# Writing out the hand-over from the up to the down product, holding late jobs behind splits, and grouping wide and narrow matmuls

## The chip, the cores and the metric

The kernel runs on one core of one Trainium2 chip. The metric is device time in microseconds: the median of three runs, 2068.24 us (2066.79 to 2068.33). The engines are named as the profile names them: PE (TensorE, with PEld for its weight loads), DVE (VectorE), ACT (ScalarE), POOL (GpSimd), and SP, whose queue issues nearly all transfers. Each engine runs its own list of instructions in order and waits on semaphores for the others.

## The reference

One residual block over 512 rows of 2048 columns in float32. What matters here is the second half, the feed-forward part:

```python
h2 = rmsnorm(x, g_mlp[l])
u = jax.nn.relu(jnp.einsum('bsd,df->bsf', h2, w_up[l]))
x = x + jnp.einsum('bsf,fd->bsd', u * u, w_down[l])
return rmsnorm(x, g_final)
```

`w_up` is 2048 x 8192 and `w_down` 8192 x 2048. Before it come an input projection, two kinds of attention with eight heads each, and an output projection.

## The kernel before, in words

**Numbers in two parts.** Every float32 operand is split into a high part (rounded to the fp32r type, a cast on ACT, L71) and a low part (the rest, a subtraction on DVE, L72). A full product is three matmuls, high by high, high by low, low by high: `mm3`, L104 to L106.

**Seven products in place of eight.** Both large matrix products use a Strassen-like scheme on 2 x 2 blocks: seven products of sums and differences of blocks, numbered 1 to 7. The sums of the weight blocks are formed on DVE in place (for the up weights L564 to L570, for the down weights L918 to L924).

**The up product** is cut into 32 units of 256 hidden columns, `Unit(u)`. Its left side F (both time halves in two parts) stays in SBUF. From unit 2 on, products 1, 2, 4, 6 and 7 join two of the three matmuls: one 512 columns wide takes high and low parts of F together against the high weights (L594), one 256 wide takes the high part of F against the low weights (L595). They stand in one loop over eight chunks, so wide and narrow alternate. Products 3 and 5 use `mm3` with 256 columns. The accumulators are the PSUM tiles `psa`, `psb`, `psc`. The copies out of them are on ACT (L622 to L627), the sums on DVE (L633 to L636), relu and square on ACT (L639, L641).

**Who sets the order.** Most of the program is ordered by a scheduler with its own estimates of time, which may move an instruction far ahead of where it is written. For the up units from 2 on, the orders on PE, ACT and DVE are written out by hand instead: a list `steps` of (unit, product) and a loop that, for each step, makes the cast for the step three ahead (L1019), the low part for two ahead (L1025), the copies and sums of the step behind, a piece of a job, and the matmuls. SP's order stays with the scheduler.

**Jobs.** The squared hidden values of a pair of units are turned into the left side of the second product by `form_steps`: a difference on DVE, a cast into a buffer `st` on ACT (L868), the low part on DVE (L870), and a store to memory `ufd` through SP (L873). Two units at the end are stored by `store_last` as `su` into `usd` (L885). `st`, `su` and `xr` share three buffers with the tag `wraw`.

**The down product** runs over eight groups of units: two of three units, six of four. In each group there are two column blocks (`db` 0 and 1), and in each the seven products in the order 1, 5, 2, 6, 3, 7, 4 (`second`). `load_b` loads four blocks of `w_down` (`wd`, L911), `load_uf` the left side of a product (`uf`, L900). A product takes its weights two units at a time: a split, then 12 matmuls for two units or 6 for one. So a product is 18 matmuls in the first two groups and 24 later. Product 1 accumulates over all groups in PSUM (`M1`, in the profile `m`). The others go into one of two `accd` buffers and from there into `M` in SBUF: by a copy on ACT in the first group (L941), by an addition on DVE in the later ones (L943). The eight residual pieces `xr` are loaded (L949), scaled on ACT (L951) and added on DVE (L952) by `add_residual`, one per column block from the fourth group on as the program is written. The stores left over (`jobs`) are written in the second group, at every other product.

**The hand-over.** Behind the written-out loop, the scheduler orders the loads for the first group, product 1 of the first column block, and products 4 and 3 of the last up unit.

Of the kernel before, what the change touches and what calls it, by code (L numbers as in the profile page):

```python
# [14 lines left out]
P = 128  # L15
NT = 512
# [10 lines left out]
NU = DFF // P // 2  # L27
# [8 lines left out]
def block_kernel(ctx, tc, x, g_attn, w_in, b_f, g_out_sb, g_out_fox, w_out, g_mlp, w_up, w_down, g_final, y):  # L36
# [505 lines left out]
    class Unit:  # L542
# [30 lines left out]
        def room(self):  # L573
            return [w.rearrange("p (a b) -> p a b", b=P) for w in hi_lo(2 * NT)]

        def parts(self, p):
            src = self.source(p)
            hi, lo = self.room()
            split(hi, lo, src)
            return hi, lo  # L580

        def multiply(self, p, parts):
# [7 lines left out]
            if self.both and p not in (5, 3):  # L590


                for a in PAIRS:
                    pe.matmul(ps, hi[:, a, :], f_both(p, a), start=a == PAIRS[0] and p == 1, stop=False, skip_group_check=True)  # L594
                    ins = pe.matmul(ps[:, 2 * P:], lo[:, a, :], f_parts(p, a)[0], start=False, stop=a == PAIRS[-1],  # L595
                                    skip_group_check=True)
                return ins
# [304 lines left out]
    def load_b(group, db):  # L902
# [9 lines left out]
                b.append(t_)  # L912
        return b

    def second(p, b, db, n, first):
        b11, b12, b21, b22 = b
        if p == 5:
# [9 lines left out]
        for u0 in range(0, n, 2):  # L927
            m = min(2, n - u0)
            hi, lo = (w.rearrange("p (a b) -> p a b", a=m) for w in hi_lo(m * NT))
            split(hi, lo, src[:, u0:u0 + m, :])  # L930
            for t in range(2):
                ts = slice(t * P, (t + 1) * P)
                for u in range(m):
                    mm3(ps[:, t, :], uf[p][:, 0, u0 + u, ts], uf[p][:, 1, u0 + u, ts], hi[:, u, :], lo[:, u, :],
                        u0 + u == 0 and (first or p != 1), u0 + u == n - 1)
        if p == 1:
            return
        if first:
# [43 lines left out]
    while squares:  # L982
# [16 lines left out]
    todo += [(q, hidden[0], 0) for q in A_ORDER]  # L999


    made = {2: Unit(2)}
    steps = [(u - i, p, n) for u in range(2, NU)
             for n, (i, p) in enumerate(((0, 1), (1, 4), (0, 5), (1, 3), (0, 6), (0, 2), (0, 7))) if u - i >= 2]
    srcs, rooms = {}, {}

    def at_step(k):
# [7 lines left out]
    def step_cast(k):  # L1015
        w, p = at_step(k)
        if w is not None and k not in rooms:
            rooms[k] = w.room()
            act.copy(rooms[k][0], srcs[k])  # L1019

    def step_low(k):
# [15 lines left out]
    with tc.manual_schedule(engines={pe.engine, act.engine, dve.engine}):  # L1037
# [5 lines left out]
        for k in range(len(steps)):  # L1043
            n = steps[k][2]
            if n == 0 and steps[k][0] + 1 < NU:
                made[steps[k][0] + 1] = Unit(steps[k][0] + 1)
            w, p = at_step(k - 1)
            if w is not None:
                w.copies(p)
# [23 lines left out]
                w.multiply(p, rooms.pop(k))  # L1073
    w, p = at_step(len(steps) - 1)
    w.finish(p)

    old = w
    for p in ORDER:
        load_uf(p, GROUPS[0])
    b_first = load_b(GROUPS[0], 0)  # L1080
    second(1, b_first, 0, GROUPS[0][1], True)
    for p in (4, 3):
        old.product(p)
    if going:
        for _ in going[0][0]:
            pass
# [34 lines left out]
    for g, group in enumerate(GROUPS):  # L1121
        last = g == len(GROUPS) - 1
        for db in range(2):
# [150 lines left out]
```

## Time and profile before

| | |
|---|---|
| median of three runs | 2068.24 us |
| profiled execution, its time | 2068.4 us |
| profiled execution, its span | 2066.7 us |
| granted TensorE clock, mean | 0.997 |
| matmuls | 10802 |
| up product with its written-out order | about 820 to 1430 us |
| hand-over | about 1410 to 1470 us |
| down product | about 1437 to 2010 us |

The page gives the busy time of each engine and the costliest groups of instructions. The answers on waits say who waited for whom; the timeline lists instructions with start and duration. A matmul's recorded duration overlaps the start of the next, so the rate of matmuls is read from starts, counts in a window, or differences between mean durations. A table of windows shows busy time and counts for PE, PEld, DVE, ACT and POOL, then the granted clock, the share of the DMA engines and their rate. The prediction shows the lines.

### The profile page before, as it was taken

What the parts mean: (1) busy time and instruction counts of PE and PEld (TensorE: products, weight loads), DVE (VectorE), ACT (ScalarE), POOL (GpSimd) and SP (SyncE); (2) the same over time, 40 slices, a digit from 0 to 9 for tenths busy, and PEclk for the clock granted to TensorE, in tenths of its full rate; (3) what the DMA queues carried; (4) which work ended last, traced back from release to release, by engine and by line L of the source; (5) the groups of instructions that cost most, each with busy time, mean ns of one, the idle gap of its engine ahead of it and who ended that gap; (6) DMA issues with size and microseconds to landing.
All of it is one profiled execution on the core that took longest, in us unless ns stands there. A gap on an engine that the chain in (4) does not pass through costs nothing.

```text
span 2066.7 us, 27642 instructions
## 1 busy us (share of the span) xinstructions
PE 2041.9 (99%) x10802; PEld 1759.7 (85%) x10802; DVE 1641.8 (79%) x1772; ACT 1092.4 (53%) x1578; POOL 54.6 (3%) x76
## 2 busy tenths in 40 slices
PE   9999999999999999999999999999999999999998
PEld 8887888888888889999999999998788888888886
DVE  6667754566578578898998999998688888989895
ACT  6434433445455466667767666676643444433443
POOL 0000000000010000000000000000000000000003
PEclk9999999999999999999999999999999999999999
DMA  7877743223238882666666666667755764764732
GB/s 246 291 273 271 254 132 83 77 87 82 71 95 264 298 261 96 210 185 186 215 200 187 210 197 191 207 197 280 264 199 198 260 238 160 279 233 144 272 115 82
DMA packets 258851, 402.46 MB, mean 195 GB/s; under 512 B 9456, under 2 KB 154912, under 8 KB 251168
## 3 DMA queue, kind: packets, MB, share of 16 engines
q1 hardware_dynamic: 257760, 398.56, 58.8%
q10 hardware_dynamic: 960, 2.13, 0.3%
q8 instruction: 85, 1.39, 0.3%
q14 instruction: 46, 0.38, 0.1%
HBM read 307.85 MB, written 92.80 MB: 194 GB/s over the span
## 4 chain that ended last, share of the span: by engine, by line
PE 82%; DMA 7%; DVE 7%; ACT 2%; issue 2%; SPq 0%; POOL 0%; ACTq 0%; DVEq 0%
PE psa L594 11%; PE accd L104 7%; PE accd L106 7%; PE accd L105 7%; PE psa L595 5%; PE accq L104 4%; PE accq L105 4%; PE accq L106 4%; PE psc L106 3%; PE psc L105 3%; PE psc L104 3%; PE psb L594 3%; DMA wsums<-mixed 2%; DMA mixed<-in_w_out_dram 2%; PE accv L104 2%
## 5 line engine op out<-in xcount | busy, mean ns | idle before, releaser
L594 PE MATMUL psa<-f,wh 128*128 128x512 f32 x728 | 258.1, 396 | 0.0
L71 ACT CAST wh<-wd 128x1024 fp32r<-128x1024 f32 (+1 forms) x136 | 134.8, 999 | 182.6 <-PE accd L106 111.7
L595 PE MATMUL psa<-f,wl 128*128 128x256 f32 x728 | 204.2, 281 | 0.0
L1025 DVE TENSOR_TENSOR wl<-wu,wh 128x1024 fp32r<-128x1024 f32 x156 | 190.1, 1218 | 14.0 <-ACT wh L1019 13.9
L104 PE MATMUL accq<-hH,wh 128*128 128x512 f32 x512 | 200.4, 391 | 0.4 <-DVE vl L75 0.4
L105 PE MATMUL accq<-hL,wh 128*128 128x512 f32 x512 | 200.2, 391 | 0.0
L106 PE MATMUL accq<-hH,wl 128*128 128x512 f32 x512 | 200.2, 391 | 0.0
L1019 ACT CAST wh<-wu 128x1024 fp32r<-128x1024 f32 x156 | 165.0, 1058 | 55.4 <-PE psc L105 41.9
L72 DVE TENSOR_TENSOR wl<-wd,wh 128x1024 fp32r<-128x1024 f32 (+1 forms) x136 | 155.3, 1152 | 41.1 <-ACT wh L71 40.7
L104 PE MATMUL accd<-wh,uf 128*128 128x512 f32 x436 | 169.8, 390 | 1.5 <-issue 0.9
L105 PE MATMUL accd<-wl,uf 128*128 128x512 f32 x436 | 169.6, 389 | 0.0
L106 PE MATMUL accd<-wh,uf 128*128 128x512 f32 x436 | 169.6, 389 | 0.0
L72 DVE TENSOR_TENSOR wl<-wraw,wh 128x1024 fp32r<-128x1024 f32 (+2 forms) x101 | 119.5, 1184 | 57.1 <-ACT wh L71 51.3
L594 PEld LDWEIGHTS psa<-f,wh 128*128 128x128 f32 x728 | 136.6, 188 | 31.4
L71 ACT CAST wh<-wraw 128x1024 fp32r<-128x1024 f32 (+2 forms) x101 | 101.8, 1009 | 107.3 <-PE accq L105 68.5
L71 ACT CAST wx<-wd 128x1024 fp32r<-128x1024 f32 (+1 forms) x88 | 87.4, 1000 | 118.5 <-PE accd L106 71.0
L595 PEld LDWEIGHTS psa<-f,wl 128*128 128x128 f32 x728 | 137.6, 189 | 0.0
L72 DVE TENSOR_TENSOR wx<-wd,wx 128x1024 fp32r<-128x1024 f32 (+1 forms) x88 | 100.9, 1153 | 23.1 <-ACT wx L71 22.7
L104 PE MATMUL accd<-wx,uf 128*128 128x512 f32 x284 | 111.6, 393 | 4.9 <-ACT m L941 4.9
L104 PEld LDWEIGHTS accq<-hH,wh 128*128 128x128 f32 x512 | 96.2, 188 | 20.3 <-PE accv L106 0.8
L106 PEld LDWEIGHTS accq<-hH,wl 128*128 128x128 f32 x512 | 96.1, 188 | 19.3
L105 PEld LDWEIGHTS accq<-hL,wh 128*128 128x128 f32 x512 | 96.2, 188 | 19.2
(367 smaller groups left out, 5373.2 us busy)
## 6 DMA issues: line engine op xcount, KB each, us to landing
wu<-in_w_up_dram SPq DMA_DIRECT2D x60, 1024.0 KB, 6.6
ufd<-st SPq DMA_DIRECT2D x98, 512.0 KB, 3.5
wd<-in_w_down_dram SPq DMA_DIRECT2D x48, 1024.0 KB, 6.7
wraw<-in_w_in_dram SPq DMA_DIRECT2D x84, 512.0 KB, 3.9
uf<-ufd SPq DMA_DIRECT2D x42, 1024.0 KB, 7.0
mixed<-in_w_out_dram SPq DMA_DIRECT2D x8, 2048.0 KB, 7.7
wsums<-mixed SPq DMA_DIRECT2D x8, 2048.0 KB, 7.2
wo<-wsums SPq DMA_DIRECT2D x28, 512.0 KB, 5.1
```

The costliest lines, as they stand in the source:

```text
L71: ins = act.copy(hi, src)
L72: lows[0] = dve.tensor_tensor(lo, src, hi.bitcast(F32), op=ALU.subtract)
L104: pe.matmul(out, sh, mh, start=first, stop=False, skip_group_check=True)
L105: pe.matmul(out, sh, ml, start=False, stop=False, skip_group_check=True)
L106: return pe.matmul(out, sl, mh, start=False, stop=last, skip_group_check=True)
L594: pe.matmul(ps, hi[:, a, :], f_both(p, a), start=a == PAIRS[0] and p == 1, stop=False, skip_group_check=True)
L595: ins = pe.matmul(ps[:, 2 * P:], lo[:, a, :], f_parts(p, a)[0], start=False, stop=a == PAIRS[-1], skip_group_check=True)
L1019: act.copy(rooms[k][0], srcs[k])
L1025: lows[0] = dve.tensor_tensor(lo, srcs.pop(k), hi.bitcast(F32), op=ALU.subtract)
```

## The change

Three edits.

1. Products 1 of the first down group and 4 and 3 of the last up unit become steps of the written-out loop: (down piece 0), (unit 31, product 4), (down piece 1), (unit 31, product 3). A small class `FirstDown` gives the two down pieces the methods that the loop calls on a unit. The loads for the first down group are issued in the loop at the first step of unit 31. The matmuls of a down piece are in a function `multiply_down` of their own.
2. `second` now remembers its cast. The late jobs of the second group and the residual pieces are issued only after the cast (on ACT) and the low part (on DVE) of the split last written.
3. The joined products run all eight wide matmuls, then all eight narrow ones.

```diff
                 for a in PAIRS:
                     pe.matmul(ps, hi[:, a, :], f_both(p, a), start=a == PAIRS[0] and p == 1, stop=False, skip_group_check=True)
+                for a in PAIRS:
                     ins = pe.matmul(ps[:, 2 * P:], lo[:, a, :], f_parts(p, a)[0], start=False, stop=a == PAIRS[-1],
                                     skip_group_check=True)
...
+    def multiply_down(ps, p, u0, hi, lo, first, last):
+        m = hi.shape[1]
+        for t in range(2):
+            ts = slice(t * P, (t + 1) * P)
+            for u in range(m):
+                mm3(ps[:, t, :], uf[p][:, 0, u0 + u, ts], uf[p][:, 1, u0 + u, ts], hi[:, u, :], lo[:, u, :],
+                    first and u == 0, last and u == m - 1)
...
-            split(hi, lo, src[:, u0:u0 + m, :])
...
+            casts[0] = split(hi, lo, src[:, u0:u0 + m, :])
+            multiply_down(ps, p, u0, hi, lo, u0 == 0 and (first or p != 1), u0 + m == n)
...
+    class FirstDown:
+
+        def source(self, i):
+            return b_first[0][:, 2 * i:min(2 * i + 2, GROUPS[0][1])]
...
+        def multiply(self, i, parts):
+            multiply_down(M1[0], 1, 2 * i, *parts, i == 0, i == 1)
...
+    made = {2: Unit(2), NU: FirstDown()}
...
+    steps += [(NU, 0, -1), (NU - 1, 4, -1), (NU, 1, -1), (NU - 1, 3, -1)]
...
+            if n == 0 and steps[k][0] + 1 == NU:
+                for p in ORDER:
+                    load_uf(p, GROUPS[0])
+                b_first = load_b(GROUPS[0], 0)
...
-    old = w
-    for p in ORDER:
-        load_uf(p, GROUPS[0])
-    b_first = load_b(GROUPS[0], 0)
-    second(1, b_first, 0, GROUPS[0][1], True)
-    for p in (4, 3):
-        old.product(p)
...
                 if g == 1 and jobs and i % 2 == 0:
-                    jobs.pop(0)()
+
+                    with tc.issue_after(casts[0].ins), tc.issue_after(lows[0].ins):
+                        jobs.pop(0)()
                 if g > 2 and pieces and i == 2:
-                    add_residual(*pieces.pop(0))
+                    with tc.issue_after(casts[0].ins), tc.issue_after(lows[0].ins):
+                        add_residual(*pieces.pop(0))
```

Line numbers in the text are those of the kernel before, unless said otherwise. In the changed kernel L594 and L596 are the wide and the narrow matmul, L1042 and L1048 the loop's cast and low part, L946 and L948 the copy into `M` and the addition, L956 the scaling of `xr`; L71 and L72, L104 to L106 keep their numbers.

PE at the end of the up product, before (`psb` is unit 31's product 2, the following `psa` its product 7, `m` the first matmul of the down product):

```order
L594 MATMUL psb<-f_6477,wh 128x512
L595 MATMUL psb<-f_6477,wl 128x256
L104 MATMUL m_0_7121<-wh,uf_13001 128x512
L594 MATMUL psa<-f_6195,wx 128x512
L595 MATMUL psa<-f_6195,wx 128x256
```

and now, from the same product 2 on:

```order
L594 MATMUL psb<-f_6190,wh 128x512 x4
L594 MATMUL psb<-f_6477,wh 128x512 x4
L596 MATMUL psb<-f_6190,wl 128x256 x4
L596 MATMUL psb<-f_6477,wl 128x256 x4
L594 MATMUL psa<-f_6195,wx 128x512 x4
L594 MATMUL psa<-f_6872,wx 128x512 x4
L596 MATMUL psa<-f_6195,wx 128x256 x4
L596 MATMUL psa<-f_6872,wx 128x256 x4
L104 MATMUL m_0_7121<-wh,uf_12809 128x512
```

Wide and narrow matmuls no longer alternate, here as in every unit from 2 on, and the down product's first matmul comes behind the whole of product 7.

ACT at the hand-over, from the copies out of `psa` for unit 31's product 4 up to the first copy into `M`, before:

```order
L626 COPY c<-psa 128x256
L627 COPY l<-psa 128x256
L71 CAST su<-c 128x512
L71 CAST wx<-wd 128x512
L71 CAST wx<-wd 128x1024
L71 CAST su<-c 128x512
L639 ACTIVATE c<-c 128x1024
L641 ACTIVATE c<-c 128x1024
L71 CAST su<-c 128x512 x2
L71 CAST wh<-wd 128x512
L941 COPY m_13143<-accd 128x2x512
```

and now:

```order
L627 COPY c<-psa 128x256
L628 COPY l<-psa 128x256
L71 CAST wh<-wd 128x1024
L71 CAST wx<-wd 128x512
L71 CAST wx<-wd 128x1024
L71 CAST wh<-wd 128x512
L640 ACTIVATE c<-c 128x1024
L946 COPY m_13143<-accd 128x2x512
L71 CAST wh<-wd 128x1024
L642 ACTIVATE c<-c 128x1024
```

The four `su` casts are gone from this place, and the copy into `M` stands ahead of the square.

DVE at the start of the second group, from the difference for product 5 (L918, now L927) to the first addition into `M`, before:

```order
L918 TENSOR_TENSOR wd<-wd 128x1536
L924 TENSOR_TENSOR wd<-wd 128x1536
L72 TENSOR_TENSOR wx<-wd,wx 128x1024
L72 TENSOR_TENSOR wx<-wd,wx 128x512
L920 TENSOR_TENSOR wd<-wd 128x1536
L72 TENSOR_TENSOR wl<-wd,wh 128x1024
L72 TENSOR_TENSOR wl<-wd,wh 128x512
L72 TENSOR_TENSOR wl<-wd,wh 128x1024
L922 TENSOR_TENSOR wd<-wd 128x1536
L72 TENSOR_TENSOR wx<-wd,wx 128x512
L943 TENSOR_TENSOR m_13143<-m_13143,accd 128x2x512
```

and now:

```order
L927 TENSOR_TENSOR wd<-wd 128x1536
L871 TENSOR_TENSOR st<-c,st 128x512
L933 TENSOR_TENSOR wd<-wd 128x1536
L72 TENSOR_TENSOR wx<-wd,wx 128x1024
L72 TENSOR_TENSOR wx<-wd,wx 128x512
L72 TENSOR_TENSOR wl<-wd,wh 128x1024
L929 TENSOR_TENSOR wd<-wd 128x1536
L72 TENSOR_TENSOR wl<-wd,wh 128x512
L72 TENSOR_TENSOR su<-c,su 128x512
L931 TENSOR_TENSOR wd<-wd 128x1536
L72 TENSOR_TENSOR wl<-wd,wh 128x1024
L72 TENSOR_TENSOR wx<-wd,wx 128x512
```

A low part of `st` and one of `su` are new in front of that addition, and a difference of 128x512 for `st` (L536) stands directly ahead of the first row; three further `su` follow behind it.

More of the change, by code (lines that the diff above doesn't have):

```diff
@@ L577, in parts @@
             src = self.source(p)
-            hi, lo = self.room()
+            hi, lo = self.room(p)
             split(hi, lo, src)
@@ L929, in second @@
             hi, lo = (w.rearrange("p (a b) -> p a b", a=m) for w in hi_lo(m * NT))
-            split(hi, lo, src[:, u0:u0 + m, :])
[L931 to L935, printed above, removed]
+            casts[0] = split(hi, lo, src[:, u0:u0 + m, :])
+            multiply_down(ps, p, u0, hi, lo, u0 == 0 and (first or p != 1), u0 + m == n)
         if p == 1:
@@ L999, in block_kernel, with room, copies @@
     todo += [(q, hidden[0], 0) for q in A_ORDER]
-    made = {2: Unit(2)}
+    class FirstDown:
+        def source(self, i):
+            return b_first[0][:, 2 * i:min(2 * i + 2, GROUPS[0][1])]
+        def room(self, i):
+            m = min(2, GROUPS[0][1] - 2 * i)
+            return [w.rearrange("p (a b) -> p a b", a=m) for w in hi_lo(m * NT)]
+        def multiply(self, i, parts):
+            multiply_down(M1[0], 1, 2 * i, *parts, i == 0, i == 1)
+        def copies(self, i):
+            pass
+        sums = copies
+    made = {2: Unit(2), NU: FirstDown()}
     steps = [(u - i, p, n) for u in range(2, NU)
              for n, (i, p) in enumerate(((0, 1), (1, 4), (0, 5), (1, 3), (0, 6), (0, 2), (0, 7))) if u - i >= 2]
+    steps += [(NU, 0, -1), (NU - 1, 4, -1), (NU, 1, -1), (NU - 1, 3, -1)]
     srcs, rooms = {}, {}
@@ L1017, in step_cast @@
         if w is not None and k not in rooms:
-            rooms[k] = w.room()
+            rooms[k] = w.room(p)
             act.copy(rooms[k][0], srcs[k])
```

2 lines of the change are left out of this document (1 added, 1 removed).

## The prediction

> **What bounds the kernel now.** I read the page first, then PE's waits, then a table of windows around the one place where PE's busy share falls, then the timeline of the engine that PE waited for.
>
> ```profile
> span 2066.7 us, 27642 instructions
> PE 2041.9 (99%) x10802; PEld 1759.7 (85%) x10802; DVE 1641.8 (79%) x1772; ACT 1092.4 (53%) x1578; POOL 54.6 (3%) x76
> ```
>
> TensorE is the bound nearly everywhere: about 25 us of the span have no matmul in flight. So a change can gain in two ways only: fill those holes, or make the matmuls themselves follow each other faster. The waits of PE say which holes are large:
>
> ```profile
> PE accd L104 <- ACT m L941: 5.4, 3, 4.1
> ...
> PE accd L104 <- issue: 0.9, 1, 0.9
> ```
>
> (Columns: total us, times, longest.) The first row is the largest: the down stage's accumulator `accd` waits three times for ScalarE's copy of an older one into `M` (L941). The windows put it in time:
>
> ```profile
> 1440.00:1450.00 10.00, 5.88 (x25) 4.55 (x24) 7.11 (x8) 6.70 (x9) 0.00 (x0) 0.89 0.73 282
> 1450.00:1460.00 10.00, 10.00 (x36) 7.88 (x34) 3.75 (x4) 4.45 (x8) 0.00 (x0) 0.77 1.00 315
> 1460.00:1470.00 10.00, 8.77 (x38) 6.75 (x37) 5.11 (x5) 8.17 (x12) 0.00 (x0) 1.00 0.64 231
> 1470.00:1480.00 10.00, 10.00 (x46) 8.28 (x45) 9.91 (x9) 6.85 (x9) 0.00 (x0) 1.00 0.30 87
> ```
>
> (Busy us and counts of PE, PEld, DVE, ACT, POOL, then granted clock, DMA share, GB/s.) An undisturbed 10 us holds 46 matmuls; between 1440 and 1460 there are 25 and 36. In the second of these PE is fully busy and still does only 36, because the granted clock is 0.77: the hole in front of it took the clock down. ScalarE shows why:
>
> ```profile
> 1430.51 0.62 ACT L868 CAST st<-c 128x512 fp32r<-128x512 f32 x1
> ...
> 1434.55 0.62 ACT L868 CAST st<-c 128x512 fp32r<-128x512 f32 x1 [2.91 <-DMA ufd<-st]
> ...
> 1443.97 0.62 ACT L71 CAST su<-c 128x512 fp32r<-128x512 f32 x1 [3.23 <-DMA ufd<-st]
> ...
> 1448.24 1.00 ACT L941 COPY m<-accd 128x1024 f32<-128x1024 f32 x1
> ...
> 1458.73 1.34 ACT L951 ACTIVATE xr<-xr,v 128x512 f32<-128x512 f32 x2 [3.30 <-DMA xr<-xd]
> 1459.98 0.99 ACT L941 COPY m<-accd 128x1024 f32<-128x1024 f32 x1
> ```
>
> ScalarE runs in order. Three instructions that nobody needs yet (`st` and `su`, pieces stored for later groups, and `xr`, a residual for the fourth group) stand ahead of the copies and wait 2.9, 3.2 and 3.3 us for a buffer or a load. The copies come late, and PE behind them.
>
> **The change, term 1: the transition.** The late jobs are now held behind the splits of their own place, so `su` and `xr` and the last `st` leave this stretch (the order rows above), and the steps around it are written out. What the stretch costs now:
>
> ```profile
> 1436.71:1470.08 33.37, 28.01 (x108) 21.96 (x109) 19.33 (x21) 20.64 (x28) 0.00 (x0) 0.90 0.80 278
> 1447.80:1454.65 6.85, 5.36 (x13) 4.20 (x14) 4.47 (x6) 4.76 (x7) 0.00 (x0) 0.50 0.82 248
> 1497.50:1555.90 58.40, 58.40 (x259) 48.37 (x258) 51.60 (x47) 23.44 (x29) 0.00 (x0) 1.00 0.64 224
> ```
>
> The third row is the same work undisturbed: 58.40/259 = 0.2255 us, or 0.227 without the two matmuls that the edges cut. The first row is 108 matmuls, six products of 18, from the first `accd` to the first matmul of the next column block: 108 x 0.227 = 24.5, taken 33.4, so **8.9 us** are lost. The two later waits stand on PE's own timeline:
>
> ```profile
> 1461.02 0.50 PE L104 MATMUL accd<-wx,uf 128*128 128x512 f32 x1 [0.79 <-ACT m L941]
> ...
> 1465.85 0.50 PE L104 MATMUL accd<-wh,uf 128*128 128x512 f32 x1 [0.44 <-ACT m L941]
> ```
>
> Of the 8.9 the first wait is 4.1, the half clock after it 13 x (5.36/13 - 0.227) = 2.4, the two later waits 0.8 + 0.4, and 1.2 are slow restarts behind the three. What the two other engines have to do for a product follows from these rows:
>
> ```profile
> L71 ACT CAST wh<-wd 128x1024 fp32r<-128x1024 f32 (+1 forms) x136 | 134.8, 999 | 182.6 <-PE accd L106 111.7
> ...
> L72 DVE TENSOR_TENSOR wl<-wd,wh 128x1024 fp32r<-128x1024 f32 (+1 forms) x136 | 155.3, 1152 | 41.1 <-ACT wh L71 40.7
> ```
>
> ```profile
> 1437.90 1.75 DVE L920 TENSOR_TENSOR wd<-wd 128x1536 f32<-128x1536 f32 x1
> ```
>
> ```profile
> 1417.41 0.52 SPq L873 DMA_DIRECT2D ufd<-st  x1
> ```
>
> I take all 8.9 away. ScalarE keeps, per product, two casts (at most 2 x 1.0) and a copy (1.0), 3.0 us of a product's 18 x 0.227 = 4.1. VectorE has two low parts (at most 2 x 1.2) and four differences of 1.75 in seven products, 3.4 of 4.1. Neither is the bound. The `st` that stays in the stretch, the one of 1430.51, takes a buffer whose store left at 1417.41 and did not wait before. Bounds: 9.3 if a hole like the smallest of the three goes at the stage switch too; 7.1 if only the large wait and its half clock go and the later ones, 1.2 with some 0.6 of restart, stay.
>
> The other half of this edit, moving the six matmuls of the second M1 piece behind product 4 of the last unit, adds and removes nothing: 18 matmuls by 0.227 in either order, their split now made by the stepper's L1019 and L1025 in place of L71 and L72. PE waited for none of them before. What covers the split is that its six matmuls now stand behind product 4's eight pairs, 2.8 us further back in PE's order. I cost it at 0; without that cover the exposed part would be one low part, 0.7 us. The seven `uf` loads and four `wd` loads are issued in nearly the same places on SP's queue, since their buffers free at the same matmuls. What is removed from SP in front of the second column block's `wd` loads is four stores and three `xr` loads; those now stand among the second group's loads, and the next `su` there stands two products, 8 us, behind the one before it, so that a buffer is free each time.
>
> On the clock the trace is plain: after a hole of 4.1 us the granted clock is 0.50 for 6.85 us, and after the holes of 0.8 and 0.4 us it stays 1.00. The Trainium skill, "TensorE: Matmul & The Clock Gate", Part 1, has the gate fall after an idle window of about 3.4 us; the trace agrees with it, and by it a remainder shorter than that would cost only itself.
>
> **Term 2: joined matmuls first.** From unit 2 on each of five products in seven issued a 512-wide matmul (both halves of F by the high weights) and a 256-wide one (low weights) in turn, eight times; now eight of the one, then eight of the other. Counts do not change. The group rows carry the price:
>
> ```profile
> L594 PE MATMUL psa<-f,wh 128*128 128x512 f32 x728 | 258.1, 396 | 0.0
> L595 PE MATMUL psa<-f,wl 128*128 128x256 f32 x728 | 204.2, 281 | 0.0
> ...
> L104 PE MATMUL accd<-wh,uf 128*128 128x512 f32 x436 | 169.8, 390 | 1.5 <-issue 0.9 <-ACT m L941 0.4
> ...
> L106 PE MATMUL psc<-f,wl 128*128 128x256 f32 x384 | 108.7, 283 | 0.0
> ...
> L594 PE MATMUL psa<-f,wx 128*128 128x512 f32 x232 | 82.2, 393 | 0.0
> ...
> L594 PE MATMUL psb<-f,wh 128*128 128x512 f32 x176 | 62.3, 393 | 0.0
> ```
>
> ```profile
> L106 PEld LDWEIGHTS psc<-f,wl 128*128 128x128 f32 x384 | 73.0, 190 | 0.0
> ```
>
> One matmul's duration overlaps the next, so only differences of these means count. Alternating, a pair is 395 (the mean of the three L594 rows by their counts) + 281; with 64 more of `psb<-f,wx` there are 1200 pairs, 150 products of eight.  A 512 behind a 512 is 390 in the down stage, a 256 behind a 256 is 283 in the `psc` products of this same stage: 673. With the unrounded means (395.1 and 280.6 over all 1200) that is 2.7 ns a pair, 1200 x 2.7 = **3.2 us** less. The starts show where it comes from:
>
> ```profile
> 907.27 0.39 PE L594 MATMUL psb<-f,wh 128*128 128x512 f32 x1
> ...
> 910.04 0.39 PE L594 MATMUL psa<-f,wh 128*128 128x512 f32 x1
> ...
> 926.95 0.40 PE L594 MATMUL psb<-f,wx 128*128 128x512 f32 x1
> ...
> 929.76 0.40 PE L594 MATMUL psa<-f,wh 128*128 128x512 f32 x1
> ```
>
> Each two are the first matmuls of neighbouring products, eight pairs apart: 2.77 us in one unit, 2.81 in the next. The alternation runs in a quicker and a slower rhythm, unit by unit. Grouped, I expect the quicker everywhere. Bounds: -4.5 us (0.03 on each of 150 products), and +2.8 us if the wide ones stay at 395 while the narrow ones rise to 283 (2.4 ns more for a pair). I take -3.2, since both replacing rows are runs of one shape, as the new order is. That PE needs the low parts 1.8 us later brings nothing: the L594 and L595 rows have 0.0 idle.
>
> **Term 3: where the jobs went.** VectorE has to do them in the second group now:
>
> ```profile
> 1430.25 0.68 DVE L536 TENSOR_TENSOR c<-c 128x512 f32<-128x512 f32 x1
> ...
> 1435.20 0.69 DVE L870 TENSOR_TENSOR st<-c,st 128x512 fp32r<-128x512 f32 x1 [0.80 <-ACT st L868]
> ...
> 1437.30 0.68 DVE L72 TENSOR_TENSOR su<-c,su 128x512 fp32r<-128x512 f32 x1
> ...
> 1507.46 1.21 DVE L943 TENSOR_TENSOR m<-m,accd 128x1024 f32<-128x1024 f32 x1
> ```
>
> ```profile
> 1498.64 0.39 PE L104 MATMUL m<-wh,uf 128*128 128x512 f32 x1
> ```
>
> One difference, one `st` and four `su`: 6 x 0.68 = 4.1 us, into a stretch where VectorE is busy 51.6 of 58.4 (third window row above), so 6.8 are free. On ScalarE it is five casts of 0.62 into 35 free. But three of the six come before the group's first addition into `M` (L943, over at 1508.7). PE needs that accumulator's bank again three products after 1498.64, at 1498.64 + 54 x 0.227 = 1510.9. The slack is 2.2 us, the added work 2.0. I allow **0.5 us** of waiting; bounds 0, and 4.1 if nothing of it is hidden. The `xr` work only moves to later groups: two scalings (1.34 for two by the `xr` row) and an addition of 1.2 at a time, in products of 24 matmuls, 5.4 us. I cost it at 0, covered by the same slack; one uncovered addition would be 1.2.
>
> **Sum.** The profiled execution took 2068.4 for its span of 2066.7; the runs' median is 2068.24, 0.2 below it. 2068.4 - 8.9 - 3.2 + 0.5 = 2056.8, in terms of the median **2056.6 us**.
>
> **Rivals.** (A) The grouped order gains nothing: the slower rhythm belongs to this stage and not to the alternation. For it: in the same stage some 256-wide rows differ by a few ns too. Against: in one unit of two the alternation already runs 0.04 us a product quicker. Time 2068.2 - 8.9 + 0.5 = 2059.8. The Trainium skill, "TensorE: Matmul & The Clock Gate", Part 2, "Back-to-back issue gap", gives each matmul a gap by its width alone, which the order cannot change; by it this rival is right, though its figures (216 and 109 ns, 325 a pair) are below the 346 to 351 that the starts above give. (B) The wait moves into the second group: VectorE's 4.1 us all exposed, and in one piece, so that the clock falls as it did, 2.4 more: 2068.2 - 8.9 - 3.2 + 4.1 + 2.4 = 2062.6; without the half clock 2060.2. For it: the slack of 2.2 against 2.0. Against: 6.8 us free over the group. (C) The other side: eight narrow matmuls in a row wait for their weights. A load's record is 190 ns and a narrow matmul leaves 120 for the next to hide in, where before every second load had a wide one to hide behind. If seven of eight wait out 70 ns, 1050 x 0.07 = 73 us, about 2130. It decides from 11.6 us / 1200 = 9.7 ns a narrow matmul. Against it stands the `psc` row: 283, three loads for three narrow matmuls in a row, with no idle. (D) The tie does not help: ScalarE still waits for a store or a load ahead of the copies. For it: the DMA engines are full there (share 1.00 from 1450 on). Against: none of the three waiting instructions stands there any more. Time 2068.2 - 3.2 = 2065.0.
>
> **How the numbers follow.** Forecast 0.74, A 0.12, B 0.06, C 0.03, D 0.05. About 0.2%, 4.1 us, is what a measurement of this kernel can tell from no change. Forecast, A and B lie beyond it: faster 0.92. D is within: same 0.05. C: slower 0.03. The range runs from 2053.8 (the best ends of terms 1 and 2 together, and 0.6 for what I have not seen) to 2062.5 (A with most of B); C, D and half of B lie outside.
>
> **What would show it.** Right: no wait of `accd` on the copy into `M` between 1430 and 1470, 46 matmuls in each 10 us there, clock 1.00; `su` casts spread over the second group; mean durations near 390 and 283 on L594 and L596. Wrong: a wait of PE on an addition into `M` near 1500 (B), means of 395 with 283 (A), narrow ones at 300 and more (C), or an ScalarE wait on a store ahead of the first copies (D).

## The result, and the profile after

| | before | after |
|---|---|---|
| median of the runs taken side by side | 2067.81 us (2066.79 to 2068.33) | 2055.61 us (2054.46 to 2056.22) |
| profiled execution, span | 2066.7 us | 2054.5 us |
| mean granted TensorE clock | 0.997 | 0.999 |

The ratio is 0.9941, with a 95% interval of 0.9924 to 0.9958: 12.2 us less, by 8.7 to 15.7. The changed kernel is faster, and the forecast of 2056.6 us is 1.0 us off.

The page of the changed kernel, its span and the busy time of its engines:

```profile
span 2054.5 us, 27634 instructions
PE 2036.2 (99%) x10802; PEld 1759.5 (86%) x10802; DVE 1641.4 (80%) x1772; ACT 1093.9 (53%) x1578; POOL 55.3 (3%) x76
```

The same 10802 matmuls are busy for 5.7 us less; the other 6.5 us are time in which no matmul was in flight. The windows show the hand-over (us, then busy us and counts of PE, PEld, DVE, ACT, POOL, then granted clock, DMA share, GB/s):

```profile
1433.34:1457.85 24.51, 24.51 (x111) 20.28 (x109) 18.61 (x18) 16.83 (x20) 0.00 (x0) 1.00 0.65 219
1440.00:1450.00 10.00, 10.00 (x46) 8.28 (x45) 6.41 (x8) 7.03 (x10) 0.00 (x0) 1.00 0.70 229
1450.00:1460.00 10.00, 10.00 (x46) 8.29 (x45) 7.86 (x7) 7.02 (x8) 0.00 (x0) 1.00 0.27 90
```

The first row answers to the 33.37 us of before: from the first `accd` to the first matmul of the next column block, 24.51 us, PE busy all of it at full clock, 46 matmuls in each 10 us. PE's waits no longer have a row of `accd` on the copy into `M`; one row of `accd` is left, the small hole in the third group that before had too (0.9 there):

```profile
PE accd L104 <- issue: 1.0, 1, 1.0
```

ScalarE's timeline at the hand-over shows why the copies (L946 now) are in time:

```profile
1437.46 1.07 ACT L640 ACTIVATE c<-c 128x1024 f32<-128x1024 f32 x1 [0.22 <-DVE c L637]
1438.43 0.99 ACT L946 COPY m<-accd 128x1024 f32<-128x1024 f32 x1
1439.32 1.05 ACT L71 CAST wh<-wd 128x1024 fp32r<-128x1024 f32 x1
1440.27 1.06 ACT L642 ACTIVATE c<-c 128x1024 f32<-128x1024 f32 x1
1441.23 0.62 ACT L71 CAST wh<-wd 128x512 fp32r<-128x512 f32 x1
1441.74 1.02 ACT L946 COPY m<-accd 128x1024 f32<-128x1024 f32 x1
...
1445.81 1.02 ACT L946 COPY m<-accd 128x1024 f32<-128x1024 f32 x1 [0.73 <-PE accd L106]
...
1449.89 1.02 ACT L946 COPY m<-accd 128x1024 f32<-128x1024 f32 x1 [0.74 <-PE accd L106]
```

No instruction waits for a store or a load. From the third copy on ScalarE waits for PE, where before PE waited for ScalarE; the copies come 4.1 us apart, a product's 18 matmuls.

**Where the 12.2 us of the two profiled spans went.** I cut the span at four starts of PE's timeline that both kernels have: the first joined product, the first `accd`, the next column block's first matmul and the second group's first.

| stretch, us | before | after | difference | predicted |
|---|---|---|---|---|
| start to the first joined product (no edit) | 839.37 | 837.44 | -1.93 | 0 |
| to the first `accd` (term 2) | 597.34 | 595.90 | -1.44 | -3.2 |
| to the next column block (term 1) | 33.37 | 24.51 | -8.86 | -8.9 |
| to the second group | 28.56 | 28.56 | 0.00 | 0 |
| to the end (term 3) | 568.04 | 568.10 | +0.06 | +0.5 |

Term 1 came as sized. Term 2 gave less than half, and 1.9 us came from a stretch that no edit touches. The experiments take both up.

### The profile page after: what moved, and what is told of

Read it like the earlier page. It is cut to its first block, busy times and chain, and to the rows that moved or that the text cites. A ratio compares the mean times of both kernels' runs of the same rounds, so it can differ in the third digit from the quotient of the medians.

```text
span 2054.5 us, 27634 instructions
## 1 busy us (share of the span) xinstructions
PE 2036.2 (99%) x10802; PEld 1759.5 (86%) x10802; DVE 1641.4 (80%) x1772; ACT 1093.9 (53%) x1578; POOL 55.3 (3%) x76
## 3 DMA queue, kind: packets, MB, share of 16 engines
q8 instruction: 85, 1.39, 0.3%
## 4 chain that ended last, share of the span: by engine, by line
PE 89%; DVE 5%; DMA 2%; ACT 1%; issue 1%; SPq 0%; POOL 0%; ACTq 0%; DVEq 0%
PE psa L594 11%; PE accd L104 7%; PE accd L105 7%; PE accd L106 7%; PE accq L105 6%; PE accq L104 6%; PE accq L106 6%; PE psa L596 6%; PE psc L106 3%; PE psc L105 3%; PE psc L104 3%; PE psb L594 3%; PE accv L104 2%; PE accv L105 2%; PE accv L106 2%; PE psb L596 1%
## 5 line engine op out<-in xcount | busy, mean ns | idle before, releaser
L71 ACT CAST wh<-wd 128x1024 fp32r<-128x1024 f32 (+1 forms) x134 | 133.5, 1003 | 177.7 <-PE accd L106 118.0
L1048 DVE TENSOR_TENSOR wl<-wu,wh 128x1024 fp32r<-128x1024 f32 x157 | 191.4, 1219 | 13.8 <-ACT wh L1042 13.8
L104 PE MATMUL accq<-hH,wh 128*128 128x512 f32 x512 | 200.4, 391 | 0.4 <-DVE vl L75 0.4
L106 PE MATMUL accq<-hH,wl 128*128 128x512 f32 x512 | 200.2, 391 | 0.0
L1042 ACT CAST wh<-wu 128x1024 fp32r<-128x1024 f32 x157 | 166.0, 1057 | 55.4 <-PE psc L105 43.3
L594 PE MATMUL psa<-f,wh 128*128 128x512 f32 x728 | 182.3, 392 | 0.0
L72 DVE TENSOR_TENSOR wl<-wd,wh 128x1024 fp32r<-128x1024 f32 (+1 forms) x134 | 153.6, 1157 | 35.5 <-ACT wh L71 35.4
L104 PE MATMUL accd<-wh,uf 128*128 128x512 f32 x436 | 169.7, 389 | 1.0 <-issue 1.0
L106 PE MATMUL accd<-wh,uf 128*128 128x512 f32 x436 | 169.6, 389 | 0.0
L72 DVE TENSOR_TENSOR wl<-wraw,wh 128x1024 fp32r<-128x1024 f32 (+2 forms) x101 | 119.8, 1187 | 56.7 <-ACT wh L71 51.0
L71 ACT CAST wh<-wraw 128x1024 fp32r<-128x1024 f32 (+2 forms) x101 | 101.8, 1009 | 111.0 <-PE accq L105 67.9
L71 ACT CAST wx<-wd 128x1024 fp32r<-128x1024 f32 (+1 forms) x88 | 87.7, 1001 | 125.2 <-PE accd L106 80.0
L594 PEld LDWEIGHTS psa<-f,wh 128*128 128x128 f32 x728 | 131.0, 189 | 23.5
L72 DVE TENSOR_TENSOR wx<-wd,wx 128x1024 fp32r<-128x1024 f32 (+1 forms) x88 | 100.9, 1154 | 23.2 <-ACT wx L71 22.9
L104 PEld LDWEIGHTS accq<-hH,wh 128*128 128x128 f32 x512 | 96.2, 188 | 20.3 <-PE accv L106 0.8
L106 PEld LDWEIGHTS accq<-hH,wl 128*128 128x128 f32 x512 | 96.1, 188 | 19.3
L104 PE MATMUL accd<-wx,uf 128*128 128x512 f32 x284 | 110.5, 389 | 0.0
L105 PE MATMUL accd<-wx,uf 128*128 128x512 f32 x284 | 110.5, 389 | 0.0
L106 PE MATMUL accd<-wx,uf 128*128 128x512 f32 x284 | 110.5, 389 | 0.0
```

The source lines that it names most:

```text
L71: ins = act.copy(hi, src)
L72: lows[0] = dve.tensor_tensor(lo, src, hi.bitcast(F32), op=ALU.subtract)
L104: pe.matmul(out, sh, mh, start=first, stop=False, skip_group_check=True)
L105: pe.matmul(out, sh, ml, start=False, stop=False, skip_group_check=True)
L106: return pe.matmul(out, sl, mh, start=False, stop=last, skip_group_check=True)
L1048: lows[0] = dve.tensor_tensor(lo, srcs.pop(k), hi.bitcast(F32), op=ALU.subtract)
```

## The experiments

Three questions: which part of the change brings the 8.9 us at the hand-over, and through which of the late jobs; what the grouping is worth, and why so little; and whether the 1.9 us in the untouched stretch belong to the change.

### One edit at a time

**Grouping alone**, on the kernel before:

```diff
                     pe.matmul(ps, hi[:, a, :], f_both(p, a), ...)
+                for a in PAIRS:
                     ins = pe.matmul(ps[:, 2 * P:], lo[:, a, :], f_parts(p, a)[0], ...)
```

> The kernel before with the third edit alone: wide matmuls first, narrow ones behind. Theory S (a change of width costs some 20 ns once per product, as the starts in the changed kernel's trace show: 2.793 us a product against 2.774 and 2.82 to 2.83 in the two rhythms of the alternation): the up stage from its first joined product to the first accd is about 1.4 us shorter (597.3 before), and the wait of accd on the copy into M stays, so the time is 1 to 2 us lower than before. Theory P (the prediction's 2.7 ns a pair): the stage is 3.2 us shorter. If the grouping also helped the hand-over, the first wait of accd would shrink from 4.1 us.

Measured: 2066.58 us against 2066.65 before, ratio 1.000 (0.9991 to 1.001): nothing. The stretch of the joined products did get shorter, 596.15 us; the hand-over behind it got longer, 36.86 us in place of 33.37. Its row in PE's waits, and three stretches of its windows:

```profile
PE accd L104 <- ACT m L942: 8.5, 2, 6.3
```

```profile
1432.51:1469.37 36.86, 28.39 (x111) 22.44 (x109) 20.77 (x23) 21.20 (x29) 0.00 (x0) 0.86 0.76 260
1443.84:1450.67 6.83, 3.49 (x8) 2.81 (x9) 3.91 (x6) 6.58 (x9) 0.00 (x0) 0.50 0.73 256
...
1460.91:1464.32 3.41, 3.41 (x9) 2.63 (x8) 1.39 (x2) 3.41 (x7) 0.00 (x0) 0.50 0.32 124
```

and ScalarE's timeline there:

```profile
1441.87 0.62 ACT L71 CAST su<-c 128x512 fp32r<-128x512 f32 x1 [4.71 <-DMA ufd<-st]
...
1446.13 1.00 ACT L942 COPY m<-accd 128x1024 f32<-128x1024 f32 x1
...
1457.17 1.33 ACT L952 ACTIVATE xr<-xr,v 128x512 f32<-128x512 f32 x2 [4.70 <-DMA xr<-xd]
1458.41 0.99 ACT L942 COPY m<-accd 128x1024 f32<-128x1024 f32 x1
```

The same kinds of instruction wait, for longer (4.7 us each where before showed 3.2 and 3.3), and the clock is halved twice instead of once. The scheduler also placed the jobs a little otherwise (before, an `st` waited 2.9 and then a `su` 3.2 us for a store; here two casts of `su` wait, 1.8 and 4.7), so the 3.5 us are not all the price of arriving earlier, and the profiled execution (2067.71) is among the longest of its ten; what the run does show is that an improvement in front of a stretch that waits for transfers need not reach the end. The 1 to 2 us that I expected of this run did not come: alone, this edit brings nothing that the timing shows.

**Everything but the grouping**, the changed kernel with the inner line taken out again:

```diff
                     pe.matmul(ps, hi[:, a, :], f_both(p, a), ...)
-                for a in PAIRS:
                     ins = pe.matmul(ps[:, 2 * P:], lo[:, a, :], f_parts(p, a)[0], ...)
```

> The changed kernel with wide and narrow matmuls alternating again, all else as changed. Theory S: the up stage takes 597.3 us again, 1.4 more than in the changed kernel; the hand-over (first accd to the next column block's first matmul) stays at 24.5 us; about 1.5 us above the changed kernel, 10 to 11 below before. Theory P: 3.2 us above it. If the grouping carried part of the hand-over's gain, that stretch would be longer than 24.5.

Measured: 2056.05 us, ratio 0.9950 (0.9935 to 0.9965). Its window from the first joined product to the first `accd`, to be read beside the same window of the changed kernel under it (two kernels, one row each):

```profile
836.08:1433.15 597.07, 597.07 (x3861) 543.34 (x3860) 548.82 (x587) 415.71 (x649) 0.00 (x0) 1.00 0.65 203
```

```profile
837.44:1433.34 595.90, 595.90 (x3861) 544.90 (x3859) 548.85 (x587) 415.60 (x649) 0.00 (x0) 1.00 0.65 203
```

PE is busy throughout in both, with the same 3861 records. So grouping is worth 597.07 - 595.90 = 1.17 us, 7.8 ns on each of 150 products, where term 2 had 21. The 1.44 of the table holds some scatter: all five experiments with the alternating order take 597.04 to 597.07 us here, only the single profile of before 597.34. The hand-over is 24.50 us with the alternating order too.

**The ties alone**, on the kernel before:

```diff
-            split(hi, lo, src[:, u0:u0 + m, :])
+            casts[0] = split(hi, lo, src[:, u0:u0 + m, :])
...
-                    jobs.pop(0)()
+                    with tc.issue_after(casts[0].ins), tc.issue_after(lows[0].ins):
+                        jobs.pop(0)()
...
-                    add_residual(*pieces.pop(0))
+                    with tc.issue_after(casts[0].ins), tc.issue_after(lows[0].ins):
+                        add_residual(*pieces.pop(0))
```

> The kernel before with the second edit alone: the late jobs and residual pieces held behind the splits, the hand-over left to the scheduler, wide and narrow alternating. Theory T (the late jobs in front of the copies are the whole cause): first accd to the next block's first matmul takes 24.5 us in place of 33.4, the clock stays at 1.00, and the time is 8 to 9 us below before. Rival W (the written-out order does it, the ties are a detail): the stretch stays at 30 us or more, because the scheduler puts something else in front.

Measured: 2056.12 us, ratio 0.9948 (0.9933 to 0.9963). The hand-over:

```profile
1432.95:1457.45 24.50, 24.50 (x111) 20.28 (x109) 18.13 (x18) 17.04 (x20) 0.00 (x0) 1.00 0.63 210
```

Two ties do all of term 1 by themselves.

**The written-out steps alone**, the changed kernel without its ties and without the grouping:

```diff
-                for a in PAIRS:
...
-                    with tc.issue_after(casts[0].ins), tc.issue_after(lows[0].ins):
-                        jobs.pop(0)()
+                    jobs.pop(0)()
...
-                    with tc.issue_after(casts[0].ins), tc.issue_after(lows[0].ins):
-                        add_residual(*pieces.pop(0))
+                    add_residual(*pieces.pop(0))
```

> The kernel before with the first edit alone: the hand-over written out, the late jobs free to be moved ahead, wide and narrow alternating. Theory T: su and xr still stand ahead of the copies on ScalarE, so the stretch from the first accd to the next block's first matmul stays well above 24.5 us (28 to 36), with a fall of the clock if one wait of PE reaches some 4 us; between 4 us faster and 2 us slower than before. Rival W: 24.5 us and 8 to 9 us below before.

Measured: 2060.94 us, ratio 0.9969 (0.9958 to 0.9981). The hand-over takes 30.35 us, 3.0 less than before. The median fell by 5.7 us, more than the trace shows there and more than the 4 us that I expected at most; the profiled execution was the longest of the seven (2063.04), so the trace may show the hand-over at its worst. PE's waits, and three windows inside the hand-over:

```profile
PE accd L104 <- ACT m L945: 3.6, 2, 2.0
```

```profile
1434.30:1464.65 30.35, 26.70 (x110) 21.26 (x109) 19.75 (x21) 20.28 (x29) 0.00 (x0) 0.94 0.88 309
...
1442.12:1445.53 3.41, 1.78 (x8) 1.15 (x7) 2.32 (x4) 3.41 (x5) 0.00 (x0) 1.00 0.51 196
1452.36:1455.77 3.41, 1.39 (x6) 0.86 (x5) 0.79 (x2) 3.41 (x6) 0.00 (x0) 1.00 1.05 404
1455.77:1459.18 3.41, 3.41 (x9) 2.64 (x8) 2.87 (x3) 2.25 (x3) 0.00 (x0) 0.50 1.04 350
```

ScalarE still waits there for a store ahead of `su` (3.78 us) and for the load of `xr` (3.36 us). So the steps help only a part, and only while the jobs are free: with the ties in place they add nothing (24.50 without them, 24.51 with them). The last window is a surprise of its own: a hole of 2.02 us ends at 1454.75, and from 1455.77 the clock is halved for 3.41 us; the hole of 1.63 us in the window before did not do that.

### Which late job

Each tie alone, on the kernel before; first the stored pieces `st` and `su`:

```diff
-            split(hi, lo, src[:, u0:u0 + m, :])
+            casts[0] = split(hi, lo, src[:, u0:u0 + m, :])
...
-                    jobs.pop(0)()
+                    with tc.issue_after(casts[0].ins), tc.issue_after(lows[0].ins):
+                        jobs.pop(0)()
```

> The kernel before with only the stores of the second group (st and su) held behind the splits; the residual pieces xr stay free. The stretch from the first accd to the next column block's first matmul took 33.4 us before and 24.5 with both ties. Theory U (su is the first wait, and xr could come early only because su had freed the shared buffers early): 24.5 us, nothing left. Rival V (each late job has its own wait): xr still stops ScalarE, 1.8 us stay, 26.3 us.

and then the residual `xr`:

```diff
-            split(hi, lo, src[:, u0:u0 + m, :])
+            casts[0] = split(hi, lo, src[:, u0:u0 + m, :])
...
-                    add_residual(*pieces.pop(0))
+                    with tc.issue_after(casts[0].ins), tc.issue_after(lows[0].ins):
+                        add_residual(*pieces.pop(0))
```

> The kernel before with only the residual pieces xr held behind the splits; the stores st and su stay free. Both theories: the first wait of accd with its fall of the clock stays (4 to 6 us of waiting, a half clock behind it), the two later waits go: the stretch takes 31 to 34 us. If xr were the larger cause, it would be below 28.

Measured in a single run each, beside 2065.64 us before: 2055.6 with the stores tied, 2065.16 with `xr` tied. The hand-over with the stores tied:

```profile
1432.45:1456.95 24.50, 24.50 (x110) 20.27 (x109) 18.14 (x18) 17.04 (x20) 0.00 (x0) 1.00 0.67 218
```

With `xr` tied, the window, PE's waits and ScalarE's timeline:

```profile
1434.01:1466.24 32.23, 27.03 (x110) 21.83 (x109) 21.62 (x23) 18.87 (x24) 0.00 (x0) 0.89 0.82 292
```

```profile
PE accd L104 <- ACT m L941: 5.2, 1, 5.2
```

```profile
1442.24 0.62 ACT L71 CAST su<-c 128x512 fp32r<-128x512 f32 x1 [4.40 <-DMA ufd<-st]
1442.77 1.05 ACT L639 ACTIVATE c<-c 128x1024 f32<-128x1024 f32 x1
1443.85 1.06 ACT L641 ACTIVATE c<-c 128x1024 f32<-128x1024 f32 x1
1444.94 1.14 ACT L71 CAST su<-c 128x512 fp32r<-128x512 f32 x2
1445.98 0.61 ACT L71 CAST wh<-wd 128x512 fp32r<-128x512 f32 x1
1446.50 1.00 ACT L941 COPY m<-accd 128x1024 f32<-128x1024 f32 x1
```

The stores are the first cause. One cast that waits 4.4 us for a buffer whose store is on its way holds back the relu, the square, three casts and the first copy, and PE behind it. With the stores tied `xr` needs no tie: ScalarE has no `xr` between 1428 and 1458 in that kernel; it was placed later there, and no run shows why the scheduler did so, or what `xr` would have cost had it stayed. Tied alone it is worth about 1 us (33.37 to 32.23). It is not harmless everywhere: in the runs of the grouping alone and of the steps alone it was the copy behind `xr` whose lateness made the holes of 2.19 and 2.02 us, with half a clock behind them.

### What the grouping costs and brings

Start times in the grouped kernel, from one matmul to the next, were not the quick rhythm. In each product the eight wide ones take 233, 236, 228, 233, 231 and then 226 to 227 ns; the first narrow one behind them takes 113 and the others 120. So a change from narrow to wide costs about 26 ns over the next five, and 6 come back at the change to narrow: 20 ns a product. Two runs test it. The first changes twice as often:

```diff
-                for a in PAIRS:
-                    pe.matmul(ps, hi[:, a, :], f_both(p, a), ...)
-                for a in PAIRS:
-                    ins = pe.matmul(ps[:, 2 * P:], lo[:, a, :], f_parts(p, a)[0], ...)
+                for some in (PAIRS[:4], PAIRS[4:]):
+                    for a in some:
+                        pe.matmul(ps, hi[:, a, :], f_both(p, a), ...)
+                    for a in some:
+                        ins = pe.matmul(ps[:, 2 * P:], lo[:, a, :], f_parts(p, a)[0], ...)
```

> The changed kernel with four wide matmuls, four narrow, four wide, four narrow in each joined product: one change from narrow to wide more per product. Theory S (a change from narrow to wide costs some 20 ns over the next four or five wide matmuls): a product takes 2.81 us in place of 2.79, the stage from the first joined product to the first accd 150 x 0.018 = 2.7 us more than in the changed kernel, 598.6 against 595.9. If the 20 ns belong to the product and not to the change of width, it stays at 595.9. The hand-over stays at 24.5 us.

The second changes less often: products 4, 6 and 7 run their narrow ones first, so that runs of one width meet at the products' borders. On PE the products of the joined kind follow each other as 6, 2, 7, 1 of the next unit, 4, with the all-narrow `psc` products in front and behind; five changes to wide in a unit become three.

```diff
+                def narrow(last):
+                    for a in PAIRS:
+                        ins = pe.matmul(ps[:, 2 * P:], lo[:, a, :], f_parts(p, a)[0], ...)
+                    return ins
+                if p in (4, 6, 7):
+                    narrow(False)
                 for a in PAIRS:
-                    pe.matmul(ps, hi[:, a, :], f_both(p, a), ...)
-                for a in PAIRS:
-                    ins = pe.matmul(ps[:, 2 * P:], lo[:, a, :], f_parts(p, a)[0], ...)
+                    ins = pe.matmul(ps, hi[:, a, :], f_both(p, a), ...)
+                if p not in (4, 6, 7):
+                    ins = narrow(True)
```

> The changed kernel with products 4, 6 and 7 running the eight narrow matmuls first and the eight wide ones behind, products 1 and 2 as changed. So a run of narrow ones meets narrow ones of the neighbouring product, and of five changes from narrow to wide per unit three are left. Theory S: 2 x 20 ns x 30 units = 1.2 us less than the changed kernel, the stage 594.7 us against 595.9, about 2054.5 by the median. If the cost belongs to the product: 595.9 and no difference. If the low parts come too late for narrow first, PE waits for the loop's low parts on VectorE and the stage is longer.

With it ran the changed kernel once more, unedited:

> The changed kernel once more, on the same chip as the one that runs back and forth. By the stages (1.4 us from the order of widths, 8.9 from the hand-over, nothing in the second group) it is 10.3 us below before; in the first comparison it was 12.2 below, of which 1.9 us lay ahead of the first joined product, where nothing was edited. Theory Z (that part is scatter between executions): 10 to 11 us below, and the unedited stretch about 836 to 838 us long. If the change acts there after all, it is 12 below again and the kernel before shows 839 there.

The same window of the three kernels, one row each: half groups, fewer changes, the changed kernel again.

```profile
835.28:1433.18 597.90, 597.90 (x3861) 544.06 (x3859) 549.00 (x587) 415.06 (x649) 0.00 (x0) 1.00 0.65 203
```

```profile
837.23:1431.93 594.70, 594.70 (x3860) 545.13 (x3859) 548.51 (x587) 415.68 (x649) 0.00 (x0) 1.00 0.65 203
```

```profile
835.90:1431.80 595.90, 595.90 (x3861) 544.94 (x3860) 548.78 (x587) 415.41 (x649) 0.00 (x0) 1.00 0.65 203
```

Half groups: +2.0 us on the changed kernel's 595.90, which makes them slower than the alternation (597.07). That is less than the 598.6 expected: the runs of four take 233, 236, 228, 233 and 235, 233, 236, 224, so each is cut off before its fifth and loses 23 and 21 ns, and the narrow ones behind them give back 9 and 2: 33 ns a product where one change costs 20, so 13 more, 2.0 us over 150. Fewer changes: -1.20, and 2 changes less in each of 30 units at 20 ns are 1.20. PE's timeline shows the price at the borders (start, duration, x matmuls in a row). First the changed kernel, then the one with fewer changes:

```profile
922.02 2.00 PE L594 MATMUL psa<-f,wh 128*128 128x512 f32 x8
923.86 1.11 PE L596 MATMUL psa<-f,wl 128*128 128x256 f32 x8
924.81 2.00 PE L594 MATMUL psb<-f,wx 128*128 128x512 f32 x8
926.65 1.12 PE L596 MATMUL psb<-f,wx 128*128 128x256 f32 x8
927.61 2.00 PE L594 MATMUL psa<-f,wh 128*128 128x512 f32 x8
```

```profile
921.65 1.12 PE L595 MATMUL psa<-f,wl 128*128 128x256 f32 x8
922.61 2.00 PE L602 MATMUL psa<-f,wh 128*128 128x512 f32 x8
924.45 1.98 PE L602 MATMUL psb<-f,wx 128*128 128x512 f32 x8
926.27 1.11 PE L595 MATMUL psb<-f,wx 128*128 128x256 f32 x8
927.22 1.12 PE L595 MATMUL psa<-f,wl 128*128 128x256 f32 x8
928.18 3.82 PE L602 MATMUL psa<-f,wh 128*128 128x512 f32 x16
```

Eight wide matmuls behind a narrow one take 1.84 us (922.02 to 923.86); eight behind a wide one take 1.82 (924.45 to 926.27).

In time the kernel with fewer changes took 2053.94 us, ratio 0.9940 (0.9926 to 0.9954); the changed kernel beside it 2055.90, ratio 0.9949 (0.9935 to 0.9963). The intervals overlap; that it is the fastest of all here rests on the 1.20 us in the traces, not on the timing.

**The untouched stretch.** The way to the first joined product took 839.37 us in the profile before and 837.44 after. PE issues the same 4238 matmuls in the same order up to there in every kernel of this study. In the nine experiments it took 835.28 to 837.23 us: 836.37 with the grouping alone and 835.91 with the ties alone on the kernel before, 835.90 when the changed kernel ran again (837.44 the first time). One program differs by 1.5 us between its two profiles, and the profile of before is the highest of eleven. The other engines, too, run the same instructions in the same order, compared up to 810 us, and the profile of before shows where its time went:

```profile
156.75 0.62 ACT L71 CAST tboth<-mixed 128x512 fp32r<-128x512 f32 x1 [6.37 <-DMA mixed<-in_w_out_dram]
```

```profile
162.28 0.50 PE L306 MATMUL ck<-ckT,nsel 128*128 128x512 f32 x1 [0.55 <-DVE ph L284]
...
191.51 0.45 PE L106 MATMUL o<-ph,vl 128*128 128x384 f32 x1 [1.27 <-DVE vl L75]
```

A load that the cast needs came 3.0 us later than in the profile after (a wait of 6.37 us against 3.38), VectorE's L284 behind it was late by as much (161.54 against 158.52), and PE waited twice, 1.82 us in all, where it does not wait in the profile after. The kernel with fewer changes, too, has the second of these waits, at 0.67 us. So I take the 1.9 us for scatter, not for a gain of the change. The kernel before was profiled once, so no run shows how often its load is late. What the edits bring in the traces is 8.86 + 1.17 = 10.0 us; the second comparison, 0.9949 of before, is 10.5.

## Why the prediction was right, and where it was not

**Term 1, the transition: right**, -8.86 against -8.9. Reading it as 108 matmuls at the undisturbed rate was enough, and each sign named for it is there: no wait, 46 matmuls, clock 1.00. The cause was narrower than told. I put the cure down to three late instructions and to steps that are written out; tying the stores alone makes it, and `xr` then follows by itself; the steps help only without the ties (3.0 us in the trace of that run, 5.7 by its median).

**Term 2, joined matmuls first: right in sign, mis-sized**, -1.2 against -3.2. The step that failed is "Grouped, I expect the quicker everywhere". I took 390 ns for the wide matmul from the down stage, where a wide one nearly always follows a wide one. In groups of eight the mean is 392:

```profile
L594 PE MATMUL psa<-f,wh 128*128 128x512 f32 x728 | 182.3, 392 | 0.0
...
L596 PE MATMUL psa<-f,wl 128*128 128x256 f32 x728 | 101.5, 282 | 0.0
```

A product takes 2.79 us (922.02 to 924.81), between the 2.77 and the 2.81 that the alternation shows; the change of width, 20 ns a product or 3.0 us over 150, is the term that my working had at nothing. By the starts the sum closes: an alternating product is on average 7.8 ns longer than a grouped one of 2.793 us, so 350.1 ns a pair; the steady rates are 226.7 + 120 = 346.7, which would give 1200 x 3.4 = 4.1 us, less 3.0 for the changes of width is 1.1, and 1.17 were measured.

**Term 3, where the jobs went: 0.0 against +0.5.** The four `su` are spread over the second group as told, though the last two casts stand one product apart (4.1 us) and not two. VectorE's first addition there, and PE's third product behind it:

```profile
1492.12 0.69 DVE L72 TENSOR_TENSOR su<-c,su 128x512 fp32r<-128x512 f32 x1
...
1496.13 1.22 DVE L948 TENSOR_TENSOR m<-m,accd 128x1024 f32<-128x1024 f32 x1
```

The addition is over at 1497.35; PE needs the bank at 1486.41 + 54 x 0.227 = 1498.7. Of the slack of 2.2 us 1.3 are left, so the added work was covered, as the bound of 0 had it.

**The sum** was 1.6 us too large for the edits (-11.6 against -10.0), and the median fell by 12.2, of which the untouched stretch may hold up to 1.9. That the forecast is 1.0 us from the median is partly luck, which lies in that stretch: by the 10.5 of the second comparison it would have been 1.1 too low, by the 10.0 of the traces 1.6.

**The rivals.** A (grouping gains nothing): its time was wrong, but it was nearer than I gave it room for; the gain is 1.2 of 3.2. A gap by width alone is not what these runs show: three orders of the same matmuls took 594.70, 595.90 and 597.90. By the formula of the Trainium skill, "TensorE: Matmul & The Clock Gate", Part 2, "Back-to-back issue gap", the order could not matter. B (the wait moves to the second group): no wait there, 28.56 us and 568.1 as before. C (narrow ones wait for weights): their mean is 282, they follow each other at 120 ns. D (the tie does not help): the ties alone make all of term 1.

**The clock.** My sentence that a remainder shorter than 3.4 us would cost only itself is wrong. In the run of the steps alone a hole of 2.02 us was followed by 3.41 us at half clock, 8 matmuls at 0.43 us in place of 0.227, another 1.6 us; in the run of the grouping alone one of 2.19 us did the same. A hole of 1.63 us left the clock at 1.00. I had also misread the trace of before: its hole began at 1445.17, and the clock fell at 1447.82, 2.65 us into it, not behind 3.4 us of idling.

What the traces show in place of that is a grid. Every stretch of one granted clock between two changes is a multiple of 3.41 us: half clock for 3.41 or 6.83, full clock between for 10.24 (3 times), 597.33 (175) or 607.57 (178). In the interval of this grid that ends with the fall, PE was idle for 2.65 us (before), 2.94 and 1.95 (grouping alone), 2.02 (steps alone) and 3.15 (`xr` tied); in the interval that held the hole of 1.63 us the clock stayed at 1.00. The second and third windows of the run of the steps alone, 1442.12 to 1445.53 and 1452.36 to 1455.77, are two such intervals: PE is busy for 1.78 and for 1.39 us of 3.41, and only behind the second does the clock fall. The full clock came back behind an interval in which PE was busy throughout. So by these traces the idle time inside one interval decides, with the limit between 1.63 and 1.95 us, and a hole of 2 to 3 us may be free or not by where it falls. No run moved a hole against the grid, so this is read from the traces and not tested. The sum was not touched, since no hole was left at the hand-over.

That the Trainium skill has the window run freely ("TensorE: Matmul & The Clock Gate", Part 1) agrees with this grid of 3.41 us; the length of idle time that it names is not a safe limit here.

## What to carry to other kernels

An instruction that nobody needs yet, on an engine that runs in order, costs nothing until its buffer or load is late; then it holds back all that stands behind it, so tie such work to the place where it was written, and look for the one instruction that waits for a transfer before rewriting the order around it. Take the price of a new order from rows with the same neighbours, not only the same shape: the borders between shapes are part of it. And compare stretches that the change does not touch first; here they moved by 1.9 us of 12.2.

## What the runs showed of the hardware that I had not expected

- A wide matmul behind a narrow one is not at its own rate at once: 233, 236, 228, 233, 231 ns for the first five of 512 columns, then 226 to 227; the first of 256 columns behind a wide one takes 113, the others 120. Why is open; no run changed the weight loads by themselves.
- The alternating order has two rhythms, 2.77 and 2.81 to 2.83 us for a product of eight pairs, which change from unit to unit. No run says what sets them.
- The granted clock changed only on a grid of 3.41 us, in every trace. It was halved for 3.41 us behind holes of 2.02 and 2.19 us, from 1.0 and 1.5 us after PE had resumed; holes of 1.63 us and less left it at 1.00. With holes of 4.1 us and more it fell inside the hole and stayed halved for 6.83 us.
